# Four RMS norms of a decoder trunk's first stage: spreading the row factors by TensorE instead of through DRAM

## The chip, the cores and the metric

The kernel runs on one core of one Trainium2 chip. The time is the device time of one execution in microseconds (us); of several runs the median is given. All times inside the program come from one profiled execution and count from the start of its span.

## The reference

A decoder of two layers on 1024 tokens of 1024 channels, in float32. Only layer 0's attention matters here:

```
hn  = x * rsqrt(mean(x*x) + eps) * attn_norm
cq  = hn @ w_dq                    # 512 channels
ckv = hn @ w_dkv                   # 256 channels and a rotary key of 64
cqn = rmsnorm(cq) * q_norm         # feeds all queries, nope and rotary
ckn = rmsnorm(ckv[:256]) * kv_norm # feeds keys and values
kpe = rope(ckv[256:], positions)
```

After that come causal attention with 8 heads, an output projection, a gated feed-forward block, then a second layer with differential attention and another such block, and a last norm.

## The kernel before

Activations lie transposed: channels on the 128 partitions, tokens along the free axis, in two halves `f` of 512 tokens. Every matmul operand is split into a high and a low part (`xh`, `xl`; `wah`, `wal`), and three matmuls make one product.

The first stage multiplies `x`, scaled by its gain only, with the joined weights of `w_dq` and `w_dkv`. For each half there is a **pass**: eight groups `k` (one for each block of 128 channels), in each of which seven accumulators (`n` = 0 to 6: four for q, two for kv, one for the rotary key) get three matmuls of 128x512, 21 in all. Four accumulators lie in the PSUM pool `mm2`, three in `bank()`. ScalarE makes `xh`, VectorE `xl`.

The norm's factor is applied behind the matmuls, since a factor for a token commutes with them. It is made thus (class `Norm`): `add` squares blocks on ScalarE and sums them in `ss` (VectorE in the first pass, GpSimd in the second); `invert` sums over partitions with small TensorE matmuls (`psn<-ones,ss`), takes the mean (`ms`) and an inverse root by ten small VectorE instructions of 128x4 (`rsy`, `rsz`, `rst`). The result `y` (shown as `rsy`) holds token j x 128 + p at partition p, column j. But it is wanted along the free axis and the same on every partition. `spread` brings it there, in one of two ways:

- `fast` false: `store` writes `y` to DRAM (`rd`), `load` reads it back to all partitions as the SBUF tile `rms`. Both DMAs are issued on the queue of SyncE.
- `fast` true: four float32 matmuls with `y`'s column broadcast as weights and the identity as the moving operand write the factor to a PSUM bank, `psr`, and the users read it there.

In the first stage six norms are made. The norms over 1024 channels of either pass, and the norms of q and kv of the first half, use the DRAM way. Only the norms of q and kv of the second half (`f == 1` in `compressed`) spread by TensorE.

With the factor `r`, `compressed` empties the seven accumulators by VectorE (`craw = acc * r`, `kraw`), adds squares for the norms of q and kv, inverts and spreads those, and makes `cn = craw * gain * rr`, split into `cqh`, `cql`, `ckh`, `ckl`. It is a generator: the first half's steps are called between the groups of the second pass (`STEP`: at k=2 q's `invert`, at k=3 kv's, at k=4 q's `spread` and `cn`, at k=5 kv's with the rotary key). The pass's own norm is inverted and spread at k=5 in the first pass and k=6 in the second (`INV`). After the second pass `rotary` multiplies the rotary query weights with `cqh`, `cql` of the first half, 48 matmuls, then the second half's norms of q and kv follow, then `rotary` for the second half, which begins the second half's use of `cqh`.

All these norms use `norm_bank`, one PSUM bank that `psn` and `psr` take in turn; the second half's q and kv use `bank`. The sine and cosine tables are made by `trig_tables` during the first pass.

The order is not written out: within `nc.start()` and `nc.finish()` all operations are recorded and then put in order by a greedy list plan (`Plan.finish`) with a duration for each operation. It picks what can start earliest, ties by place in the code. This order is fixed when the program is built; on the chip each engine runs its own list in order. The later stages have plans of their own. Almost every instruction is issued by one helper, so the profile shows it as line L287, and tile names tell them apart.

Of the kernel before, what the change touches and what calls it, by code (L numbers as in the profile page):

```python
# [11 lines left out]
F32 = mybir.dt.float32  # L12
F32R = mybir.dt.float32r
I32 = mybir.dt.int32
AF = mybir.ActivationFunctionType
# [5 lines left out]
P = 128  # L21
D = 1024
S = 1024
HF = 512
# [346 lines left out]
def trunk(ctx: ExitStack, tc: tile.TileContext, A: dict):  # L371
    nc = Plan(tc)
# [16 lines left out]
    def gain(which, k):  # L389
        c = GAINS[which] + k  # L390
        return gains[:, c : c + 1]
# [9 lines left out]
    def bank(name="ps"):  # L401
        if nc.on:
            return nc.ask(banks[0], [P, HF], F32, name, banks[1].get(name))
        return mm.tile([P, HF], F32, name=name, tag="mm")
# [4 lines left out]
    def move(dst, src):  # L409
        nc.sync.dma_start(out=f32(dst), in_=f32(src))  # L410

    def split(dst_hi, dst_lo, src, scale=1.0, sub=None):
        nc.scalar.activation(dst_hi, src, AF.Copy, scale=scale)
        if isinstance(scale, float) and scale == 1.0:
            (sub or nc.vector).tensor_tensor(dst_lo, src, f32(dst_hi), ALU.subtract)
        else:
            nc.vector.scalar_tensor_tensor(dst_lo, src, scale, f32(dst_hi), ALU.mult, ALU.subtract)
# [45 lines left out]
    def early(place):  # L463
        return xa if place[0] == "x" else z1
# [8 lines left out]
    class Norm:  # L473
# [34 lines left out]
        def spread(self):  # L508
            if self.fast:
                r = self.bank("psr")  # L510
                for j in range(self.n):
                    nc.tensor.matmul(r[:, j * P : (j + 1) * P], lhsT=self.y[:, j : j + 1].to_broadcast([P, P]), rhs=ident, start=True, stop=True)
                return r
            return self.load(self.store(), self.tmp)

# [26 lines left out]
    with tc.using_default_side("right"):  # L542
# [8 lines left out]
    tmpa = Tags(lambda q: {"ss": norma, "r": norma, "craw": crawp, "t": norma}.get(q) or (wa_p if q[0] == "w" else early(q)), kraw=("z5",), ss=("ss",), r=("r",), craw=("craw",),  # L551
                t=("z6", "z7", "z8", "z9", "t", "t"), xh=[q + "h" for q in spare], xl=[q + "l" for q in spare],
                y=[f"wa{part}{k}" for k in range(4, 8) for part in "hl"], rot=[q + part for q in spare for part in "hl"])
# [57 lines left out]
    def causal_mask():  # L611
        nc.gpsimd.memset(mask, 0.0)
        nc.gpsimd.affine_select(
            out=mask[:, S - P :], in_=mask[:, S - P :], pattern=[[-1, P]], base=0, channel_multiplier=1,
            compare_op=ALU.is_ge, fill=NEG,
        )
# [4 lines left out]
    def load_x(f, k):  # L621
        x = xs.tile([P, HF], F32, name="x", tag="x")
        nc.sync.dma_start(out=x, in_=A["x"][f, k])
        return x
# [21 lines left out]
    def compressed(f, acc, r):  # L646


        tok = slice(f * HF, (f + 1) * HF)
        kinds = (("q", Q_LORA, 0, NQ, cqh, cql), ("kv", KV_LORA, NQ, NC_, ckh, ckl))  # L650
        norms, raws = [], []
        for which, dim, lo_n, n_t, _, _ in kinds:
            norms.append(Norm(tmpa, dim, fast=f == 1, bank=bank if f else norm_bank))
            for n in range(lo_n, lo_n + n_t):
                c = tmpa.tile([P, HF], F32, name="craw", tag="craw", bufs=6)
                nc.vector.tensor_tensor(c, acc[n], r, ALU.mult)
                norms[-1].add(c)
                raws.append(c)
        kraw = tmpa.tile([P, HF], F32, name="kraw", tag="kraw")
        nc.vector.tensor_tensor(kraw, acc[NA - 1], r, ALU.mult)  # L660
        for norm in norms:
            yield
            norm.invert()
        for norm, (which, _, lo_n, n_t, dst_h, dst_l) in zip(norms, kinds):
            yield
            rr = norm.spread()
            for n in range(n_t):
                t = tmpa.tile([P, HF], F32, name="cn", tag="t")
                nc.vector.scalar_tensor_tensor(t, raws[lo_n + n], gain(which, n), rr, ALU.mult, ALU.mult)
                split(dst_h[n][f], dst_l[n][f], t)  # L670
        m1 = tmpa.tile([P, HF], F32, name="m1", tag="t")
        m2 = tmpa.tile([P, HF], F32, name="m2", tag="t")
        nc.vector.tensor_tensor(m1[0:64], kraw[0:64], cs[0:64, tok], ALU.mult)
        nc.vector.tensor_tensor(m2[0:64], kraw[64:128], cs[64:128, tok], ALU.mult)
        nc.vector.tensor_tensor(m1[0:64], m1[0:64], m2[0:64], ALU.add)
        split(krh[0:64, tok], krl[0:64, tok], m1[0:64])
        for t in (krh, krl):
            move(t[64:128, tok], t[0:64, tok])
        yield
# [62 lines left out]

    for f in range(2):
        acc = [mm2.tile([P, HF], F32, name="acc", tag="mm2") for _ in range(4)] + [bank() for _ in range(3)]
        norm = Norm(tmpa, D, adder=nc.gpsimd if f else nc.vector, bank=norm_bank)
        after = []
        for k in range(KT):
            if (f, k) == TRIG:
                c4, s4, cs = trig_tables()
                causal_mask()  # L750
            if (f, k) in STEP:
                next(before, None)
            x = xt[k]
            xh = tmpa.tile([P, HF], F32R, name="xh", tag="xh")
            xl = tmpa.tile([P, HF], F32R, name="xl", tag="xl")
            split(xh, xl, x, scale=gain("attn0", k))
            for i in range(0 if k == 0 else k + LEAD, min(k + LEAD + 1, KT)):
                norm.add(xt[i])
            if k == INV[f]:
                norm.invert()  # L760
                r = norm.spread()
            if f == 0:
                after.append(load_x(1, k))
            for n in range(NA):
                cols = slice(n * P, (n + 1) * P)
                nc.tensor.matmul(acc[n], lhsT=wa_h[k][:, cols], rhs=xh, start=k == 0, stop=False)
                nc.tensor.matmul(acc[n], lhsT=wa_h[k][:, cols], rhs=xl, start=False, stop=False)
                nc.tensor.matmul(acc[n], lhsT=wa_l[k][:, cols], rhs=xh, start=False, stop=k == KT - 1)
        for _ in before:
            pass  # L770
        xt = after
        before = compressed(f, acc, r)
        next(before)
    ws = [rotary_weights(g) for g in range(2)]
# [1205 lines left out]
```

## Time and profile before

| | |
|---|---|
| median of 3 runs | 2520.44 us (2517.12 to 2521.76) |
| profiled execution | 2517.07 us |
| its span | 2515.0 us |
| its mean granted TensorE clock | 0.977 |
| matmuls busy | 2335.8 us |
| VectorE, ScalarE, GpSimd busy | 1929.2, 1164.3, 1125.1 us |

The first stage takes about the first 160 us of the span. Busy shares are means over the whole span; what holds a stage is read from its own waits and its own timeline. TensorE, VectorE, ScalarE and GpSimd are called PE, DVE, ACT and POOL in the rows, PEld is TensorE's weight load, and SPq is the queue of SyncE.

### The profile page before, as it was taken

How to read it: one execution, taken by the hardware profiler on the slowest of the kernel's cores; microseconds unless marked ns; L12 is line 12 of the kernel's file. 1: busy time of each engine (PE TensorE's matmuls, PEld its weight loads, DVE VectorE, ACT ScalarE, POOL GpSimd, SP SyncE). 2: the span in 40 equal slices, each digit the busy share in tenths (PEclk: the TensorE clock that was granted, in tenths of full speed). 3: DMA queues.
4: the chain of work that ended last, by engine and by line, in shares of the span. 5: the costliest groups of instructions: out<-in, count | busy, mean ns of one | idle time of the engine just before them, and what ended most of it. 6: DMA issues, size and time to landing. Idle time of an engine off the chain costs nothing. (4 is left out here: it accounts for less than half of the span.)

```text
span 2515.0 us, 38090 instructions
## 1 busy us (share of the span) xinstructions
PE 2335.8 (93%) x12744; PEld 1996.4 (79%) x12744; DVE 1929.2 (77%) x3685; ACT 1164.3 (46%) x2319; POOL 1125.1 (45%) x979
## 2 busy tenths in 40 slices
PE   8689999999899998999999999989989999988997
PEld 6579988778788886777788888878768888876777
DVE  6575555387887789999678677676598787789997
ACT  4246555244444444344355555554344444454442
POOL 2145652163555554123377674444264555542212
PEclk9899999999999998999999999999999999999999
DMA  5156665566332235332266663373744232244322
GB/s 182 22 158 203 197 199 177 163 214 202 111 92 72 84 104 179 92 105 92 87 201 198 207 196 113 106 233 125 251 142 154 79 93 72 85 147 149 103 66 73
DMA packets 204691, 347.41 MB, mean 138 GB/s; under 512 B 26832, under 2 KB 59856, under 8 KB 204496
## 3 DMA queue, kind: packets, MB, share of 16 engines
q1 hardware_dynamic: 204496, 344.99, 43.8%
q8 instruction: 101, 1.65, 0.3%
q14 instruction: 94, 0.77, 0.1%
HBM read 240.94 MB, written 95.04 MB: 134 GB/s over the span
## 5 line engine op out<-in xcount | busy, mean ns | idle before, releaser
L287 ACT ACTIVATE wh<-wr 128x512 fp32r<-128x512 f32 (+2 forms) x530 | 287.5, 550 | 450.1 <-PE pb L287 137.7
L287 DVE TENSOR_TENSOR wl<-wr,wh 128x512 fp32r<-128x512 f32 (+2 forms) x530 | 396.0, 761 | 38.6 <-ACT wh L287 38.0
L287 PE MATMUL pa<-xh,wh 128*128 128x512 f32 (+1 forms) x850 | 339.6, 401 | 35.9 <-DVE h L287 16.2
L287 PE MATMUL pa<-xh,wl 128*128 128x512 f32 (+1 forms) x850 | 337.3, 398 | 18.4 <-DVE wl L287 17.1
L287 PE MATMUL pa<-xl,wh 128*128 128x512 f32 (+1 forms) x850 | 336.6, 396 | 4.0 <-DVE xl L287 4.0
L287 PE MATMUL pb<-xh,wh 128*128 128x256 f32 (+1 forms) x976 | 293.7, 304 | 23.4 <-DVE s L287 17.4
L287 PE MATMUL pb<-xl,wh 128*128 128x256 f32 (+1 forms) x976 | 293.0, 301 | 0.0
L287 PE MATMUL pb<-xh,wl 128*128 128x256 f32 (+1 forms) x976 | 291.8, 301 | 0.0
L287 POOL TENSOR_TENSOR wr<-wr 128x512 f32<-128x512 f32 x128 | 179.6, 1403 | 172.6 <-DMA wr<-wgu 84.3
L287 POOL TENSOR_TENSOR xl<-stg,xh 128x512 fp32r<-128x512 f32 x66 | 110.9, 1698 | 305.3 <-ACT xh L287 159.0
L287 PEld LDWEIGHTS pa<-xh,wh 128*128 128x128 f32 x850 | 163.0, 192 | 77.5 <-DVE h L287 14.6
L287 PEld LDWEIGHTS pb<-xh,wh 128*128 128x128 f32 x976 | 187.6, 193 | 46.2 <-DVE s L287 26.6
L287 PEld LDWEIGHTS pa<-xh,wl 128*128 128x128 f32 x850 | 162.1, 191 | 57.0 <-DVE wl L287 24.8
L287 PEld LDWEIGHTS pb<-xl,wh 128*128 128x128 f32 x976 | 188.5, 193 | 13.7
L287 PEld LDWEIGHTS pb<-xh,wl 128*128 128x128 f32 x976 | 188.0, 193 | 6.0 <-DVE wl L287 0.5
L287 PEld LDWEIGHTS pa<-xl,wh 128*128 128x128 f32 x850 | 163.0, 192 | 34.4 <-DVE xl L287 5.7
L287 POOL TENSOR_SCALAR p<-p,tot 128x640 f32<-128x640 f32 (+7 forms) x128 | 98.9, 774 | 180.6 <-DVE tot L287 114.0
L287 ACT ACTIVATE p<-sc,nmax 128x128 f32<-128x128 f32 (+7 forms) x192 | 141.8, 740 | 77.6 <-DVE nmax L287 45.3
L287 POOL TENSOR_TENSOR qt<-wr 128x256 f32<-128x256 f32 x120 | 102.8, 876 | 124.8 <-DVE wl L287 107.2
L287 DVE TENSOR_TENSOR s<-s,pb 128x256 f32<-128x256 f32 (+1 forms) x278 | 115.6, 426 | 39.5 <-PE pb L287 36.6
L287 PE MATMUL pc<-xh,wh 128*128 128x512 f32 x352 | 139.1, 398 | 4.5 <-DVE h L287 4.3
L287 PE MATMUL pc<-xl,wh 128*128 128x512 f32 x352 | 138.9, 395 | 2.5 <-DVE xl L287 2.5
(295 smaller groups left out, 6491.2 us busy)
## 6 DMA issues: line engine op xcount, KB each, us to landing
wr<-wgu SPq DMA_DIRECT2D x142, 256.0 KB, 3.2
act_d<-s SPq DMA_DIRECT2D x88, 256.0 KB, 2.5
stg<-act_d SPq DMA_DIRECT2D x88, 256.0 KB, 2.9
wr<-wd SPq DMA_DIRECT2D x96, 192.0 KB, 2.4
pb<-wgu SPq DMA_DIRECT2D x60, 256.0 KB, 4.0
preh<-ph SPq DMA_DIRECT2D x58, 256.0 KB, 3.0
prel<-pl SPq DMA_DIRECT2D x58, 256.0 KB, 2.8
wh<-preh SPq DMA_DIRECT2D x58, 256.0 KB, 4.8
```

Of the source, the lines that this page charges most:

```text
L287: return getattr(getattr(self.nc, engine), name)(*map(put, args), **{k: put(a) for k, a in kw.items()})
```

## The change

`spread` gets a third way, `fast="sbuf"`: the four matmuls of the TensorE way, then one ScalarE copy of `psr` into the SBUF tile `rms`, which has the tag and the two buffers that `load` used. The four norms of the first stage that went through DRAM take this way. Users of `rms` are as they were. The norms of the second half's q and kv stay with `psr`, and no other stage's norm is touched.

```diff
                 r = self.bank("psr")
                 for j in range(self.n):
                     nc.tensor.matmul(r[:, j * P : (j + 1) * P], lhsT=self.y[:, j : j + 1].to_broadcast([P, P]), rhs=ident, start=True, stop=True)
+                if self.fast == "sbuf":
+                    t = self.tmp.tile([P, HF], F32, name="rms", tag="r", bufs=2)
+                    nc.scalar.activation(t, r, AF.Copy)
+                    return t
                 return r
             return self.load(self.store(), self.tmp)
...
-            norms.append(Norm(tmpa, dim, fast=f == 1, bank=bank if f else norm_bank))
+            norms.append(Norm(tmpa, dim, fast=True if f else "sbuf", bank=bank if f else norm_bank))
...
-        norm = Norm(tmpa, D, adder=nc.gpsimd if f else nc.vector, bank=norm_bank)
+        norm = Norm(tmpa, D, fast="sbuf", adder=nc.gpsimd if f else nc.vector, bank=norm_bank)
```

## Rows read from the trace of the kernel before

**Rows 1.** The page: busy time, and TensorE's granted clock in 40 slices.

```profile
PE 2335.8 (93%) x12744; PEld 1996.4 (79%) x12744; DVE 1929.2 (77%) x3685; ACT 1164.3 (46%) x2319; POOL 1125.1 (45%) x979
...
PEclk9899999999999998999999999999999999999999
```

**Rows 2.** View of waits, 30 to 160 us: total, times, longest.

```profile
DVE craw L287 <- DMA rms<-rd: 21.2, 2, 12.6
...
DVE cn L287 <- DMA rms<-rd: 14.4, 2, 11.1
```

**Rows 3.** Timeline of the queue of SyncE: start, us, what.

```profile
76.58 0.39 SPq L287 DMA_DIRECT2D rd<-rsy  x1
84.97 0.33 SPq L287 DMA_DIRECT2D rms<-rd  x1
85.39 0.38 SPq L287 DMA_DIRECT2D rd<-rsy  x1
97.03 0.32 SPq L287 DMA_DIRECT2D rms<-rd  x1
```

**Rows 4.** Timeline of VectorE; idle time before in brackets.

```profile
40.47 0.16 DVE L287 TENSOR_TENSOR rsy<-rsy,rsz 128x4 f32<-128x4 f32 x1
...
53.76 2.48 DVE L287 TENSOR_TENSOR craw<-acc,rms 128x512 f32<-128x512 f32 x4 [8.59 <-DMA rms<-rd]
...
75.42 1.13 DVE L287 TENSOR_TENSOR rsy<-rsy,rsz 128x4 f32<-128x4 f32 x1
...
80.57 0.16 DVE L287 TENSOR_TENSOR rsy<-rsy,rsz 128x4 f32<-128x4 f32 x1
91.88 2.74 DVE L287 SCALAR_TENSOR_TENSOR cn<-craw,gains,rms 128x512 f32<-128x512 f32 x4 [11.15 <-DMA rms<-rd]
...
100.85 1.42 DVE L287 SCALAR_TENSOR_TENSOR cn<-craw,gains,rms 128x512 f32<-128x512 f32 x2 [3.22 <-DMA rms<-rd]
...
103.01 0.75 DVE L287 SCALAR_TENSOR_TENSOR xl<-x,gains,xh 128x512 fp32r<-128x512 f32 x1
...
121.17 2.48 DVE L287 TENSOR_TENSOR craw<-acc,rms 128x512 f32<-128x512 f32 x4 [12.60 <-DMA rms<-rd]
```

**Rows 5.** Timeline of TensorE; idle time before in brackets.

```profile
54.59 0.77 PE L287 MATMUL acc<-xh,wah 128*128 128x512 f32 x1 [6.53 <-DVE craw L287]
...
58.55 0.39 PE L287 MATMUL acc<-xh,wah 128*128 128x512 f32 x1
...
61.81 0.40 PE L287 MATMUL ps<-xh,wal 128*128 128x512 f32 x1
...
66.24 1.00 PE L287 MATMUL psn<-ones,ss 128*128 128x64 f32 x8
...
103.82 0.80 PE L287 MATMUL acc<-xl,wah 128*128 128x512 f32 x1 [10.02 <-DVE xl L287]
...
109.85 0.39 PE L287 MATMUL ps<-xh,wah 128*128 128x512 f32 x1
...
122.01 0.77 PE L287 MATMUL psr<-cqh,wrh 128*128 128x512 f32 x1 [10.61 <-DVE craw L287]
...
126.81 0.39 PE L287 MATMUL psr<-cqh,wrl 128*128 128x512 f32 x1
...
138.24 1.16 PE L287 MATMUL psr<-ident,rsy 128*128 128x128 f32 x8 [0.85 <-DVE rsy L287]
139.69 1.13 PE L287 MATMUL psr<-ident,rsy 128*128 128x128 f32 x8 [0.29 <-DVE rsy L287]
141.99 1.20 PE L287 MATMUL psr<-cqh,wrh 128*128 128x512 f32 x4 [1.17 <-ACT cqh L287]
```

**Rows 6.** ScalarE: groups by form (busy us, mean ns, idle us before), then its timeline.

```profile
L287 ACT ACTIVATE kh<-psp 128x512 fp32r<-128x512 f32 x16 | 9.5, 597 | 10.2 <-PE psp L287 10.2
...
54.48 0.63 ACT L287 ACTIVATE ss<-craw 128x512 f32<-128x512 f32 x1 [9.90 <-DVE craw L287]
```

**Rows 7.** Timeline of GpSimd.

```profile
71.12 7.26 POOL L287 TENSOR_TENSOR ss<-ss,sq 128x512 f32<-128x512 f32 x5
```

## The prediction

> **What bounds the kernel now.** I read the page first: TensorE's matmuls are busy for 93% of the span, and its granted clock is below nine tenths in only two of 40 slices, the second being the one from 63 to 126 us [rows 1]. So the first stage differs from the rest. The view of waits names who is late there: VectorE's `craw` and `cn` wait 21.2 and 14.4 us for the load `rms<-rd` [rows 2]. The reader is to see one pattern three times in the timelines.
>
> First pass (token half 0): the inverse root `rsy` is ready at 40.47 + 0.16 = 40.63 us, and `craw`, its first user, starts at 53.76 us after 8.59 us of idle VectorE, released by `rms<-rd` [rows 4]. That is 13.1 us for a trip to DRAM and back. TensorE ended the pass at 54.59 - 6.53 = 48.06 us and stood still, since the next pass needs the accumulators that `craw` empties [rows 5].
>
> Norms of q and kv: the queue of SyncE issues store, load, store, load in order, at 76.58, 84.97, 85.39 and 97.03 us [rows 3]. A load can't start until its store has landed, 8.4 and 11.6 us later, and kv's store stands behind q's load, though kv's `rsy` was ready at 80.73 us. `cn` of q starts at 91.88, that of kv at 100.85, and queued behind them on VectorE is the `xl` of 103.01 that TensorE wants: idle 10.02 us [rows 4, 5].
>
> Second pass: the same trip once more, `craw` at 121.17, TensorE idle 10.61 us from 111.40 [rows 4, 5].
>
> After each gap matmuls come at half rate. Warm ones are (61.81 - 58.55)/14 = 0.233 us apart. After the gaps, nine take 54.59 to 58.55 (1.86 us more than 9 x 0.233), fourteen take 103.82 to 109.85 (2.77 more), eleven take 122.01 to 126.81 (2.24 more) [rows 5]. In these stretches TensorE is on the path that sets the end: idle and half rate are 27.16 + 6.87 = 34.0 us.
>
> **The change, part by part.** It removes four stores and four loads on SyncE's queue, and with them the trip from `rsy` to `rms`. It adds for each of the four norms four matmuls (recorded as eight) and one ScalarE copy PSUM to SBUF. The second half's q and kv norms already spread by TensorE: one spread of eight records took 1.16 us [rows 5]. The copy has no row of its own; a ScalarE copy of 128x512 out of PSUM into fp32r took 597 ns on average [rows 6]. So `rms` is there about 1.16 + 0.60 + 0.1 for hops = 1.9 us after `rsy`, not 13.1. The users still read SBUF, so their durations don't change. Nothing is moved by hand, but the stage's order is planned anew.
>
> The copies (4 x 0.6 = 2.4 us) I cost at nothing: ScalarE works in order and has gaps where they stand, such as 9.90 us before 54.48 [rows 6]. If that cover failed they would delay `craw` and `cn` by 0.6 us each, which delays TensorE only where an accumulator or an `xl` is then late. The norm bank of PSUM is a single one; each spread now holds it until its copy ends, 1.8 us, and the next user (a sum of squares one group, 21 x 0.233 = 4.9 us, on) comes later than that. The spreads on TensorE are not hidden: 1.16 each, bounds 1.13 to 1.16 by the two rows.
>
> The new wait: TensorE works in order, so a spread that stands in its queue before `rsy` is ready stops all matmuls behind it. Row by row:
>
> First norm: the nearest rows are the two spreads of the second half, for which TensorE waited 0.85 and 0.29 us [rows 5]. Mean 0.6, bounds 0 to 1.3.
>
> q: its sum of squares is on TensorE at 66.24 us, at the start of group k=2; `rsy` is ready at 75.42 + 1.13 = 76.55, 10.3 us later [rows 4, 5]. The code puts the spread at k=4, behind two groups and two sums: 2 x (4.9 + 1.0) = 11.8 us. Margin 1.5, so wait 0. kv: ready at 80.73, 14.5 us later; its spread stands at 11.8 + 1.16 + 4.9 = 17.9. Wait 0. Bounds for both together: 0 to 3.4.
>
> q's chain is slow because GpSimd adds squares at the same time (5 adds from 71.12 in 7.26 us): a 128x4 instruction that takes 0.16 us at 80.57 took 1.13 at 75.42 [rows 4, 7], and about every other one is slow, five of the ten. That speaks against the change, since TensorE is now behind this chain. The Trainium skill, "SBUF — State Buffer", section "Who interferes with whom", says that VectorE and GpSimd share a port pair by an exclusive lock, and who comes second blocks for the whole instruction. By that rule every instruction of the chain could lose an add's time; here only every other one did, so the trace agrees in part.
>
> Fourth norm (second pass): sum at k=6, when the adds are over; wait 0.6 as for the first, bounds 0 to 1.3. Its `rms` comes in time: `craw` needs the first accumulator's last matmul, about one group later.
>
> What is late next. First pass: `craw` 0 waits for its accumulator, whose last matmul is 18 x 0.233 = 4.2 us before the pass ends, so `craw` runs under the matmuls and no gap is left: 6.53 + 1.86 - 1.16 - 0.6 = 6.6 us gained. Second pass: the `cn` run soon after each spread, under matmuls, and the `xl` of k=7 is no longer behind a DMA: 10.02 + 2.77 - 3 x 1.16 - 0.6 = 8.7 us. After the second pass: today 111.40 to 141.99, 30.6 us, lie between its end and the first matmul that needs the second half's `cqh` [rows 5], of which 20.8 follow the start of `craw` at 121.17. With `craw` starting 4.2 us before the end, that matmul comes 20.8 - 4.2 = 16.6 us after it. TensorE's own work in between is 48 x 0.233 (rotary of the first half) + about 2 (sums) + 2.3 (spreads) = 15.5, so 16.6 stands: 30.6 - 16.6 = 14.0 gained. Bounds: 9.8 if the `craw` don't start until the pass ends, 15.1 if TensorE's work alone counts.
>
> Sum: 6.6 + 8.7 + 14.0 = **29.3 us**. By the bounds: (5.9 to 7.2) + (5.3 to 9.3) + (9.8 to 15.1) = 21 to 31.6. What follows starts from these results and has no clock of its own (one core runs alone), so it moves up as a whole. The profiled execution took 2517.07 us (span 2515.0): 2517.07 - 29.3 = 2487.8. The median of the runs is 3.4 higher, 2520.44, which gives 2491.1. I forecast **2490 us**, between them, nearer the median.
>
> **Rivals.** (a) *TensorE waits for the slowed chain.* If all ten instructions of q's chain are slow, five more by 1.0 us, `rsy` is ready 15.3 us after the sum against 11.8: wait 3.5, and kv's behind it some 2. With a further wait of that size at the fourth norm the gain is 20 to 25: 2495 to 2500. For it: the 1.13 us row. Against: the every-other pattern leaves a margin of 1.5. By the rule of "SBUF — State Buffer" in the Trainium skill, named above, this would be the case to expect. (b) *VectorE becomes the wait.* From q's sum to the end of the second pass, six groups or some 36 us with sums and spreads, it has to put the chains of q and kv with what lies between (14.5), six `cn` (2.74 us for four [rows 4], so 4.1), their six differences (about as much) and some 7 us for the fourth chain, `xl` and the rotary key. Should the plan put `xl` behind `cn` late again, or the fourth `rsy` come late, half of the second or third term stays: gain 12 to 20, 2500 to 2508. Against: that is about 30 of 36 us. (c) *No effect*: another input than `rms` would have come as late. Against: each wait in [rows 2] names the load, and the accumulators were done 5.7 us before `craw`. Gain under 5. (d) *Slower.* The new plan puts each spread right behind its own sum. Then TensorE stands through each chain: 76.55 - 67.24 = 9.3 us as for q, and goes to half rate, 2.8 more, 12.1 a norm and 48 for four, against 34.0 - 4.6 = 29.4 gained: 2539. It decides once the waits pass 29.4 us, 7.4 a norm. Against: the code asks for q's and kv's spreads two groups later, and the spreads in today's trace waited under 1 us.
>
> **How the numbers follow.** Forecast (gain 25 to 33) 0.70; (a) 0.13; (b) 0.10; (c) 0.03; (d) 0.04. About 0.2%, 5 us, is what a measurement of this kernel tells from no change. Faster: 0.70 + 0.13 + 0.10 and a little of (c), 0.94; same 0.03; slower 0.03, as (d) could end even. Range: from a gain of 33 on the profiled execution, 2484, through (a) into (b), a gain of 18 on the median, 2502.
>
> **What would show it.** No `rd` in the trace; four more groups of eight `psr<-ident,rsy`, and four ScalarE copies of about 0.6 us. No TensorE gap over 1.5 us between 12 and 95 us, full clock from 40 to 110 us; the second pass ending near 96 us, the first matmul on the second half's `cqh` near 113, not 141.99. Stages after it unchanged in length. I am wrong if TensorE shows idle time before `psr<-ident,rsy` of several us (a, d), if `xl` or `craw` still hold it (b), or if a later stage gives the time back.

## The result, and the profile of the changed kernel

The changed kernel took 2488.66 us, median of four runs (2486.97 to 2491.85), against 2520.43 us (2517.12 to 2521.76) for the kernel before on the same chip: a ratio of 0.9877, with a 95% interval from 0.986 to 0.9894. The forecast was 2490 us. By the medians the gain is 31.8 us, by the interval 26.7 to 35.3. The profiled execution took 2489.24 us, 27.8 us less than that of before, which at 2517.07 us is the fastest of its executions; so a comparison of the two profiles shows somewhat less than the medians do.

The page of the changed kernel, busy time and granted clock, against [rows 1]:

```profile
PE 2334.4 (94%) x12776; PEld 1998.5 (80%) x12776; DVE 1928.1 (78%) x3685; ACT 1167.5 (47%) x2323; POOL 1124.2 (45%) x979
...
PEclk9999999999999999999999999999999999999999
```

TensorE has 32 matmuls more (four spreads of eight records), ScalarE four instructions more, and the weak slice of the clock from 63 to 126 us is gone. (The other weak slice of before, from 943 to 1006 us, is gone too; it lies far behind this stage, and nothing here says why.) Busy times hardly moved: what went is idle time. Two of the six stores `rd<-rsy` are left, both in later stages (the forecast's sign, no `rd` at all, overlooked them), so no norm of this stage goes through DRAM. TensorE's timeline shows where the four spreads stand and what replaced the gaps of [rows 5] (start, us, what; idle time before in brackets):

```profile
40.20 1.05 PE L287 MATMUL psr<-ident,rsy 128*128 128x128 f32 x8
...
48.79 0.40 PE L287 MATMUL acc<-xh,wah 128*128 128x512 f32 x1
...
58.59 1.00 PE L287 MATMUL psn<-ones,ss 128*128 128x64 f32 x8
...
70.17 1.05 PE L287 MATMUL psr<-ident,rsy 128*128 128x128 f32 x8
70.97 0.48 PE L287 MATMUL acc<-xh,wah 128*128 128x512 f32 x1
71.29 0.40 PE L287 MATMUL acc<-xl,wah 128*128 128x512 f32 x1
...
75.96 1.05 PE L287 MATMUL psr<-ident,rsy 128*128 128x128 f32 x8
...
86.86 1.13 PE L287 MATMUL psr<-ident,rsy 128*128 128x128 f32 x8 [0.56 <-DVE rsy L287]
...
94.13 0.40 PE L287 MATMUL psr<-cqh,wrh 128*128 128x512 f32 x1
...
110.67 1.19 PE L287 MATMUL psr<-cqh,wrh 128*128 128x512 f32 x4
```

The second pass begins at 48.79 us and follows the first without a gap. The row of 94.13 us is the first matmul after the second pass, and that of 110.67 us the first on the second half's `cqh`. The one wait left is 0.56 us. The table by windows of the changed kernel (busy us of each engine, granted clock, DMA) says the same:

```profile
40.00:60.00 20.00, 20.00 (x96) 16.42 (x95) 12.10 (x23) 12.73 (x22) 0.00 (x0) 1.00 0.52 113
60.00:80.00 20.00, 20.00 (x100) 16.64 (x99) 19.44 (x36) 6.94 (x12) 9.85 (x7) 1.00 0.00 1
80.00:100.00 20.00, 19.44 (x94) 15.77 (x93) 14.57 (x33) 6.25 (x10) 0.00 (x0) 1.00 0.06 14
100.00:120.00 20.00, 20.00 (x102) 16.47 (x102) 19.56 (x49) 6.35 (x11) 5.08 (x4) 1.00 0.28 106
```

TensorE (first number behind the comma) is busy but for that wait, at the full clock (1.00, the upper of its two levels, 2.4 GHz), from 40 to 120 us. The new copies on ScalarE, then on VectorE the last instruction of q's root, the `craw` of the second pass and a user of TensorE's `psr` behind it:

```profile
41.30 0.60 ACT L287 ACTIVATE rms<-psr 128x512 f32<-128x512 f32 x1 [2.27 <-PE psr L287]
...
71.28 0.58 ACT L287 ACTIVATE rms<-psr 128x512 f32<-128x512 f32 x1
...
77.66 0.58 ACT L287 ACTIVATE rms<-psr 128x512 f32<-128x512 f32 x1
...
88.09 0.60 ACT L287 ACTIVATE rms<-psr 128x512 f32<-128x512 f32 x1 [4.57 <-PE psr L287]
```

```profile
67.77 1.13 DVE L287 TENSOR_TENSOR rsy<-rsy,rsz 128x4 f32<-128x4 f32 x1
...
90.20 2.72 DVE L287 TENSOR_TENSOR craw<-acc,rms 128x512 f32<-128x512 f32 x4 [3.49 <-PE acc L287]
...
99.93 0.69 DVE L287 TENSOR_TENSOR t<-psr,s 128x512 f32<-128x512 f32 x1 [1.51 <-PE psr L287]
```

`craw` of the second pass now waits for its accumulator, not for the load of [rows 4].

### The profile page after: what moved, and what is told of

Read it like the earlier page. It is cut to its first block, busy times and chain, and to the rows that moved or that the text cites. A ratio compares the mean times of both kernels' runs of the same rounds, so it can differ in the third digit from the quotient of the medians.

```text
span 2487.0 us, 38148 instructions
## 1 busy us (share of the span) xinstructions
PE 2334.4 (94%) x12776; PEld 1998.5 (80%) x12776; DVE 1928.1 (78%) x3685; ACT 1167.5 (47%) x2323; POOL 1124.2 (45%) x979
```

## The experiments

The code behind attention's start is the same in all kernels but e11, which changes one pair of instructions of the second head; yet the time from the fifth store of attention's output to the end of the span ran from 2295 to 2310 us in their profiled executions. So effects of a few us are read at three landmarks: the first matmul on the second half's `cqh`, the first matmul of attention's scores (`sc<-kh,qh`), and the fifth store of attention's output (`o_hi<-oh` on the queue of SyncE). They are the same work in every kernel. What TensorE has done before the first of them is not: in the changed kernel and in e1, e4, e5, e7, e8, e10 and e11 seven matmuls of the first head's projections stand ahead of it, in e9 two, in before, e2, e3 and e6 none. Starts in us, then the ratio to the kernel before on the same chip with its interval:

| kernel | `cqh` | score | fifth store | ratio |
|---|---|---|---|---|
| before | 141.99 | 161.48 | 219.82 | |
| changed | 110.67 | 130.84 | 191.22 | 0.9877 (0.986 to 0.9894) |
| e1, pass norms only | 126.15 | 146.31 | 204.87 | 0.9933 (0.9909 to 0.9957) |
| e2, q and kv only | 128.67 | 148.15 | 206.69 | 0.9932 (0.9913 to 0.9951) |
| e3, first pass only | 137.43 | 156.93 | 215.19 | 0.9968 (0.9954 to 0.9982) |
| e4, before with gaps filled | 141.38 | 161.56 | 221.19 | 1.0005 (0.9991 to 1.0019) |
| e5, spreads early | 115.90 | 136.07 | 194.40 | 0.9898 (0.9879 to 0.9917) |
| e6, e5 with VectorE's adds | 110.65 | 130.72 | 189.05 | 0.9879 (0.9862 to 0.9896) |
| e7, no copy for q and kv | 111.44 | 131.62 | 188.94 | 0.987 (0.9856 to 0.9885) |
| e8, low half by VectorE | 111.78 | 130.93 | 191.87 | 0.9865 (0.9848 to 0.9881) |
| e9, other buffers | 110.52 | 130.49 | 190.03 | 0.9865 (0.9838 to 0.9891) |
| e10, changed once more | 111.44 | 131.62 | 189.63 | 0.9864 (0.9844 to 0.9884) |
| e11, high half by GpSimd | 110.36 | 130.56 | 189.10 | 0.9869 (0.9839 to 0.99) |

**One part at a time.** e1 keeps the new way for the two pass norms and gives q and kv of the first half back to DRAM; e2 does the opposite; e3 keeps it for the first pass alone.

```diff
 e1, e3
-            norms.append(Norm(tmpa, dim, fast=True if f else "sbuf", bank=bank if f else norm_bank))
+            norms.append(Norm(tmpa, dim, fast=f == 1, bank=bank if f else norm_bank))
 e2
-        norm = Norm(tmpa, D, fast="sbuf", adder=nc.gpsimd if f else nc.vector, bank=norm_bank)
+        norm = Norm(tmpa, D, adder=nc.gpsimd if f else nc.vector, bank=norm_bank)
 e3
+        norm = Norm(tmpa, D, fast="" if f else "sbuf", adder=nc.gpsimd if f else nc.vector, bank=norm_bank)
```

> The two norms over 1024 channels spread by TensorE with a copy, the norms of q and kv of the first half go through DRAM again. Theory (each trip stood on TensorE's path by itself): only the middle gap comes back, 9.6 us by the trace after the change, so about 2498 us and one gap of about 10 us before the k=7 xl. Rival (the trips lean on each other through the orders of the engines): the fourth spread now stands in TensorE's order ahead of that xl, its rsy is queued on VectorE behind the late cn of kv, and TensorE stops there instead, for about 12 us and the half rate after it: 2502 us, the gap before psr<-ident,rsy.

> The norms of q and kv spread by TensorE, the two norms over 1024 channels go through DRAM as before. Theory: the first gap comes back in full (7.7 us). The last one comes back only in part, since rsy of the second pass is ready some 7 us before that pass ends and no longer behind the late cn: a trip of 12.5 us leaves a gap of about 5 instead of 10.6, and craw runs behind it, which costs 9.5 us; together 17 us, 2506 us. Rival (each trip has its own fixed price): 7.7 + 14 back, 2510 us.

> Only the norm of the first pass spread by TensorE, the other three through DRAM. Theory: the first gap and its half rate go, less one spread, 7.7 us by the trace after the change: 2512.7 us, with the middle and last gaps at 10 and 10.6 us as before. Rival (the gain of the first pass is swallowed by the next wait in line, the trip of q and kv): under 3 us, 2518 us or more.

In e1 TensorE's one long wait stands ahead of the fourth spread, and VectorE's timeline says why:

```profile
101.83 2.04 PE L287 MATMUL psr<-ident,rsy 128*128 128x128 f32 x8 [16.42 <-DVE rsy L287]
```

```profile
93.97 1.42 DVE L287 SCALAR_TENSOR_TENSOR cn<-craw,gains,rms 128x512 f32<-128x512 f32 x2 [6.00 <-DMA rms<-rd]
...
101.53 0.16 DVE L287 TENSOR_TENSOR rsy<-rsy,rsz 128x4 f32<-128x4 f32 x1
```

The chain of the second pass's norm is queued behind kv's `cn`, which still waits for its load; it ends at 101.53 + 0.16 = 101.69 us, and TensorE stands for 16.42 us. So a late kv holds the pass norm's spread as well, as the rival had it. The size agrees with the rival too: at the fifth store e1 is 13.65 us behind the changed kernel, where the rival's time stands for some 13 and the theory's for 9.6.

In e2 the two outer gaps are back and the middle one is gone; the loss at the fifth store, 15.5 us, is nearer to the theory's 17 than to the rival's 21.7. Of it 1.4 us are trips that took longer than in before (13.62 and 13.53 us from root to `craw`, against 13.13 and 12.60). The theory's last gap had the wrong size: the root was ready 5.9 us before the pass ended, not 7, and the gap is 8.40 us, not 5:

```profile
54.91 0.77 PE L287 MATMUL acc<-xh,wah 128*128 128x512 f32 x1 [6.64 <-DVE craw L287]
...
108.86 0.79 PE L287 MATMUL psr<-cqh,wrh 128*128 128x512 f32 x1 [8.40 <-DVE craw L287]
```

At the fifth store e1 gains 14.95 us and e2 13.13, together 28.1 of the 28.6 us of both (at the `cqh` landmark 29.2 of 31.3): within what the trips vary, the two halves of the change add up. e3 gains 4.6 us. q's sum of squares, which stands ahead of its first remaining trip, and kv's `cn` behind that trip:

```profile
59.80 1.00 PE L287 MATMUL psn<-ones,ss 128*128 128x64 f32 x8
```

```profile
95.42 1.42 DVE L287 SCALAR_TENSOR_TENSOR cn<-craw,gains,rms 128x512 f32<-128x512 f32 x2 [5.81 <-DMA rms<-rd]
```

At q's sum e3 is 66.24 - 59.80 = 6.4 us ahead of before, the changed kernel 7.7 us; the difference is the wait ahead of the first spread, 1.34 us in e3 and none in the changed kernel. Behind it e3's trips took 1.7 us longer than those of before: 21.15 us from kv's root to its `cn` against 20.12, and 13.26 us from the last root to `craw` against 12.60. So the first pass alone is worth 6.4 to 7.7 us, and the next trips do not swallow it, against the rival; they were only longer in this execution. By the median time e3 gains 8 us (4.5 to 11.6).

**The half rate after the gaps.** Behind the first and the last gap of before the granted clock is 0.50 (54.6 to 58.5 and 122.1 to 126.8 us), the lower of its two levels, 1.2 GHz: the half rate. e4 is the kernel before with useless matmuls into `norm_bank` behind each pass (24 and 40), so that TensorE is busy during most of the first and last gap.

```diff
+        fill = norm_bank("fill")
+        for i in range((24, 40)[f]):
+            nc.tensor.matmul(fill, lhsT=wa_h[KT - 1][:, :P], rhs=xh, start=True, stop=True)
```

> The kernel before, with all four trips through DRAM, and matmuls of no use put behind the first pass (24 of 128x512) and the second pass (40), so that TensorE works through most of the two gaps; nothing is left out. Theory (of the 34 us, 1.86 and 2.24 us are the half rate after these two gaps, the rest is the wait for the trip): the gaps stay as long, the matmuls after them come 0.233 us apart at once, 2516 us. Rival (the half rate is the greater part of what the change gives back): more than 8 us faster than before. If the filling itself delays the passes, slower than before.

```profile
48.01 5.76 PE L287 MATMUL fill<-xh,wah 128*128 128x512 f32 x24
55.21 0.47 PE L287 MATMUL acc<-xh,wah 128*128 128x512 f32 x1 [1.43 <-DVE craw L287]
...
111.56 9.50 PE L287 MATMUL fill<-xh,wah 128*128 128x512 f32 x40
123.22 0.56 PE L287 MATMUL psr<-cqh,wrh 128*128 128x512 f32 x1 [2.16 <-DVE craw L287]
```

After the first gap the full rate is there at once (granted clock 1.00 from 55.3 to 59.0 us), after the second it is not (0.43 us from matmul to matmul up to 126.57 us, granted clock 0.52 from 123.3 to 126.5). VectorE's timeline, first of before, then of e4, shows that the half rate after the last gap does cost something:

```profile
130.04 1.29 DVE L287 TENSOR_TENSOR t<-psr,s 128x512 f32<-128x512 f32 x2 [1.58 <-PE psr L287]
```

```profile
122.38 2.48 DVE L287 TENSOR_TENSOR craw<-acc,rms 128x512 f32<-128x512 f32 x4 [13.31 <-DMA rms<-rd]
...
130.64 0.69 DVE L287 TENSOR_TENSOR t<-psr,s 128x512 f32<-128x512 f32 x1 [0.38 <-PE psr L287]
```

In before VectorE stands 1.58 us for a `psr` that TensorE's matmuls at half rate finish late; in e4, with a shorter stretch at half rate, 0.38 us. The first matmul on the second half's `cqh` follows `craw` by 141.38 - 122.38 = 19.0 us, against 20.8 in before [rows 4, 5]; a part of that is the new order of e4, since the first score comes no earlier. Behind the first gap, from `craw` to q's root, e4 takes 21.6 us against 22.8. But the trips were longer in this execution (13.70 against 13.13 us from the first root to `craw`, 21.26 against 20.12 from kv's root to its `cn`, 13.31 against 12.60 ahead of the last `craw`), 2.4 us together, and whether the added matmuls have to do with that is not shown. In the time no gain is to be seen: the ratio is 1.0005, and its interval, 0.9991 to 1.0019, excludes the theory's gain of 4 us as well as the rival's of more than 8. So the half rate is a small part of what the change gives back, up to 1.2 us behind the first gap and 1.8 behind the last in the trace, and none of it shows in the time.

**Where the spreads stand.** e5 asks for q's and kv's spread right behind the inverse root, in place of two groups later; e6 does that and also lets VectorE add the second pass's squares, so that GpSimd is idle there.

```diff
 e5, e6
+            norm.rr = None if f else norm.spread()
...
-            rr = norm.spread()
+            rr = norm.spread() if f else norm.rr
 e6
-        norm = Norm(tmpa, D, fast="sbuf", adder=nc.gpsimd if f else nc.vector, bank=norm_bank)
+        norm = Norm(tmpa, D, fast="sbuf", bank=norm_bank)
```

> As after the change, but the spreads of q and kv of the first half are called right behind their inversion, two groups earlier in the code. Theory (a spread that stands in TensorE's order before rsy is ready stops all matmuls behind it, and rsy of q takes 10.3 us from its sum because GpSimd adds squares meanwhile): the plan puts q's spread 20 matmuls behind its sum, 5.5 us, so TensorE waits about 5 us there, perhaps with 2 us of half rate: 2494 to 2496 us. Rival (the place in the code does not matter, the wait is hidden by slack later in the stage): within 2 us of the changed kernel, 2487 to 2491.

> As e5, but VectorE, not GpSimd, adds the squares of the second pass, so that GpSimd is idle during the chains of q and kv. Theory (GpSimd's adds are what makes every other 128x4 instruction take 1.1 us): all ten instructions of q's chain take 0.15 to 0.17 us, rsy of q is ready before its spread, no gap there: 2488 to 2491 us. Rival (the slow instructions are slow by themselves, or VectorE's own seven adds of 0.6 us cost as much): 1.1 us instructions are still there, or the gap before the spread is, 2494 us or more.

TensorE and VectorE in e5:

```profile
58.30 1.00 PE L287 MATMUL psn<-ones,ss 128*128 128x64 f32 x8
...
68.67 2.04 PE L287 MATMUL psr<-ident,rsy 128*128 128x128 f32 x8 [4.65 <-DVE rsy L287]
```

```profile
64.52 0.16 DVE L287 TENSOR_TENSOR rst<-rst,rsz 128x4 f32<-128x4 f32 x1
64.72 1.11 DVE L287 SCALAR_TENSOR_TENSOR rsy<-rst,rsy 128x4 f32<-128x4 f32 x1
```

TensorE stands 4.65 us, the spread itself runs at half rate (granted clock 0.50 from 69.0 to 71.5 us), and the second half's `cqh` comes 5.2 us later than in the changed kernel. In e6 there is no wait, and the chain's instructions, from 62.44 to 68.48 us, take 0.15 or 0.16 us each:

```profile
70.07 1.05 PE L287 MATMUL psr<-ident,rsy 128*128 128x128 f32 x8
```

```profile
64.62 0.15 DVE L287 TENSOR_TENSOR rst<-rst,rsz 128x4 f32<-128x4 f32 x1
...
65.35 0.15 DVE L287 SCALAR_TENSOR_TENSOR rsy<-rst,rsy 128x4 f32<-128x4 f32 x1
```

So GpSimd's adds make the slow instructions: 1.11 us beside them, 0.15 us without. But e6 is not clean on TensorE's wait. Its plan knew of VectorE's adds, which stand between the chain's instructions, and put the spread 10.7 us after the sum's start, not 5.7. The root is ready 9.3 us after the sum's start there (68.48 + 0.15 - 59.38) and 10.2 us in e5 (67.42 + 1.10 - 58.30): as the rival expected, VectorE's own adds cost almost as much. Of the wait of 4.65 us the faster chain thus accounts for about 1 us; it is the place of the spread that took the rest away. The Trainium skill, "SBUF — State Buffer", section "Who interferes with whom", says that VectorE and GpSimd share a port pair by an exclusive lock, and that VectorE instructions with two SBUF inputs, or in a two-port mode, contend for it. That the slow rows come with GpSimd's adds agrees; that the same `rst<-rst,rsz` with two inputs takes 0.16 us beside them does not follow from it, so the trace agrees in part.

**The copy.** In e7 q's and kv's `cn` read the factor from PSUM, without ScalarE's copy.

```diff
-            norms.append(Norm(tmpa, dim, fast=True if f else "sbuf", bank=bank if f else norm_bank))
+            norms.append(Norm(tmpa, dim, fast=True, bank=bank if f else norm_bank))
```

> As after the change, but the norms of q and kv of the first half are spread without the ScalarE copy: cn reads the factor from PSUM. Theory (the copy is off the path): cn takes 0.74 us either way, but the one norm bank is held until the last cn of q, about 1 us after kv's spread could start, so TensorE waits about 1 us: 2488 to 2491 us, no measurable change. Rival (the copy's 0.6 us and its hops are on the path): 2 to 3 us faster than the changed kernel, 2486.

```profile
77.47 1.13 PE L287 MATMUL psr<-ident,rsy 128*128 128x128 f32 x8 [1.09 <-DVE cn L287]
```

The bank is held until `cn` has read it, and kv's spread waits 1.09 us. The second half's `cqh` comes 52.6 us after q's sum (58.85 to 111.44), against 52.1 in the changed kernel and in its repeat e10: 0.5 us later, not the 2 to 3 us earlier of the rival, and no difference in time can be measured. The copy costs nothing that shows here, and it frees the bank.

**The start of attention.** 31.3 us gained at the `cqh` landmark have become 28.6 us at the fifth store. Four kernels look for the rest. In the changed kernel TensorE waits 1.94 us for GpSimd's low half of the first head's key weights, then runs at half rate (granted clock 0.50 from 127.8 to 129.0 us):

```profile
126.21 0.50 PE L287 MATMUL psp<-ckh,wlo 128*128 128x512 f32 x1 [1.94 <-POOL wlo L287]
...
127.77 0.63 PE L287 MATMUL psp<-ckh,whi 128*128 128x512 f32 x1
...
146.24 0.39 PE L287 MATMUL psv<-whi,ckh 128*128 128x256 f32 x1 [1.84 <-DVE vl L287]
...
148.66 0.63 PE L287 MATMUL sc<-kh,qh 128*128 128x512 f32 x1
```

e8 makes that low half on VectorE, e9 puts the weights in buffers that are free earlier, and e10 is the changed kernel again, without an edit.

```diff
 e8
...
-        st["wk"] = weight(A["wuk"][0], NC_ * P, "k")
+        st["wk"] = weight(A["wuk"][0], NC_ * P, "k", sub=nc.vector)
 e9
+        st["wk"] = weight(A["wuk"][0], NC_ * P)
```

> As after the change, and the low part of the first head's key weights, made just before attention, is taken by VectorE instead of GpSimd, which is the wait of 1.94 us that TensorE has at 126 us of the changed trace, before a stretch at half rate. Theory (that wait is on the path): the gap there goes, and with it some of the half rate, 2 to 4 us faster than the changed kernel, 2485 to 2487 us. Rival (VectorE, busy 19.6 of 20 us from 100 to 120, is late instead): no change, 2488 to 2490.

> The changed kernel, with the high and low half of the first head's key weights in another pair of buffers, which nothing of the first stage occupies, so that TensorE need not wait for GpSimd's low half (1.94 us at the projection that uses it) when it starts that head's keys. What is looked at is when the fifth store of attention's output stands on SyncE's queue, 219.82 us before and 191.22 us in the changed kernel. Theory: the wait of 1.94 us and the half rate behind it are the place where about 2.8 us of the gain are given back; without them the fifth store comes at 187 to 189.5 us, and the time is 2485 to 2489 us, which is within the spread of the rest of the kernel. Rival: the wait moves to the next thing that TensorE needs (the rotated queries or keys, or the low half again, since GpSimd makes it behind the same work as before); the store stays at 190 to 192 us.

> The changed kernel once more, without an edit. Theory: what is given back at the start of attention depends on short waits there after which TensorE falls to half rate or not, and this differs between executions; the fifth store of attention's output, at 191.22 us in the first trace, comes anywhere between 188.5 and 191.5 us. Rival: it is fixed by the order of the instructions; the store comes at 191.2 us within 0.3 us, with the same two waits ahead of it. For either the time is 2484 to 2495 us and the ratio to the kernel before 0.985 to 0.990.

e8 waits 2.76 us for VectorE's `wlo`; its first score follows the `cqh` landmark by 19.15 us, 1.0 us less than in the changed kernel (20.17), but the fifth store is no earlier. e9 has no wait there, but 3.48 us for ScalarE's `qh` ahead of the first score, which comes 0.35 us earlier. In both the rival is right as far as the fifth store goes: the next thing is late. Nor does the half rate behind this wait set the first score: in e5 and e11, which run the projections behind the same wait at full rate, the stretch is 20.17 and 20.20 us. e10 decides more than they do: the same instructions in the same order gave the fifth store 1.6 us earlier, at 189.63 us, with 0.85 us of waiting ahead of the `psv` row, not 1.84, and no half rate behind it. The rival, that the order alone fixes it, falls.

What times the `psv` row is in ScalarE's timeline; the row of e10, which comes to this place 0.8 us later and finds the load landed at the same time, stands under that of the changed kernel:

```profile
144.16 0.63 ACT L287 ACTIVATE whi<-wraw 128x512 fp32r<-128x512 f32 x1 [2.14 <-DMA wraw<-wuqn]
144.69 0.67 ACT L287 ACTIVATE p<-sc,nmax 128x512 f32<-128x512 f32 x1
```

```profile
144.12 0.64 ACT L287 ACTIVATE whi<-wraw 128x512 fp32r<-128x512 f32 x1 [1.16 <-DMA wraw<-wuqn]
```

ScalarE waits there for the second head's query weights, and a softmax row (144.69) and the copy `vh` (145.36), from which VectorE makes `vl`, are queued behind. That `psv` follows the `whi` row by 2.08 us in the changed kernel (144.16 to 146.24) and in before (174.30 to 176.38), by 2.09 in e10 and by 2.08 to 2.09 in e1, e2, e3, e5, e6, e7 and e8; in e4 and e9 TensorE shows no wait there. The load takes 7.3 us from its issue (136.86) in the changed kernel, 6.45 in e10 and 6.8 in before. e11 takes ScalarE out of this:

```diff
...
-                st["wq"] = weight(A["wuqn"][h], NQ * P)
+                st["wq"] = weight(A["wuqn"][h], NQ * P, hi=nc.gpsimd if h == 1 else None)
```

> The changed kernel, with the high part of the second head's query weights made by GpSimd and not by ScalarE, so that in ScalarE's queue no instruction that waits for that load's landing (144.16 us in the changed kernel, 144.12 in its repeat) stands ahead of a softmax row and of the copy that the first value projections need. Theory: in nine traces the value projection that waits follows ScalarE's first use of this load by 2.08 to 2.09 us, so the landing of the load is what times this place; with the use moved, that projection no longer stands 2.1 us behind the landing, its wait (1.84 and 0.85 us) is gone, and the fifth store of attention's output comes at 187.5 to 189.5 us, not 189.6 to 191.2. Rival: the pairing is a coincidence of the order, and what times the place is VectorE's or GpSimd's own work there; the value projection waits as before or GpSimd, which now stands behind the load, holds the softmax rows that it scales; the store comes at 189.6 us or later. The time is 2485 to 2495 us for either.

ScalarE's and TensorE's timelines in e11:

```profile
141.03 0.69 ACT L287 ACTIVATE p<-sc,nmax 128x512 f32<-128x512 f32 x1
...
146.10 0.63 ACT L287 ACTIVATE ph<-pt 128x512 fp32r<-128x512 f32 x1 [3.46 <-DMA preh<-ph]
```

```profile
142.53 0.28 PE L287 MATMUL psv<-whi,ckh 128*128 128x256 f32 x1
...
147.81 0.38 PE L287 MATMUL psv<-whi,ckh 128*128 128x256 f32 x1 [1.77 <-DVE vl L287]
```

The softmax row comes 3.7 us earlier than in the changed kernel and the value projections no longer wait for the load, as the theory said. But ScalarE then waits 3.46 us for another transfer, `preh<-ph`, and TensorE 1.77 us for the next `vl`. The fifth store, 189.10 us, is within the theory's range, 2.1 us earlier than in the changed kernel but only 0.5 earlier than in e10. So a transfer that ScalarE's queue stands behind does time this place; when one is taken away, the next does. That this is worth anything at the fifth store is not shown, since two executions of the changed kernel differ there by 1.6 us. No version beats the changed kernel by what can be measured: the intervals of e6 to e11 all contain its ratio.

## Why the prediction was right

The forecast of 2490 us holds, and so does the mechanism in the main; two of its steps came out right partly by luck. By its own steps:

- **The trip.** In the first pass the root is ready at 39.82 + 0.15 = 39.97 us and `rms` at 41.30 + 0.60 = 41.90 us: 1.9 us, as forecast, against 13.1 by DRAM.
- **First term, 6.6 us forecast, 7.7 measured.** The tenth matmul of the second pass moved from 58.55 [rows 5] to 48.79 + 9 x 0.233 = 50.89 us. The wait of 0.6 us did not occur in this execution. Of the ten traces with this spread five show no wait there and five one of 0.97 to 1.40 (the repeat e10 1.32, which leaves it 6.9 us at q's sum); so the bounds of 0 to 1.3 were about right, and 0.6 was a mean between two outcomes. The spread was priced too high: the matmul behind it starts 0.8 us after it, as at 70.17 and 70.97, and comes back to the 0.233 pace 0.09 later, so a spread costs TensorE about 0.9 us, not the 1.16 of its record. The records of pipelined matmuls overlap.
- **Second term, 8.7 forecast, 9.6 measured** (111.40 - 94.13 = 17.3, less 7.7). Three spreads at 0.9 in place of 1.16 give 0.8 of the difference. q and kv did not wait: q's root is ready at 68.90 us, its spread stands at 70.17, a margin of 1.3 us where 1.5 was worked out. The fourth norm waited 0.56, forecast 0.6. (The term's lower bound is not summed as its parts say: with both waits at their upper bounds, 3.4 and 1.3, it is 4.6, not 5.3, and the gain's 20, not 21. Nothing hangs on it.)
- **Third term, 14.0 forecast, 14.0 measured.** From the end of the second pass to the first matmul on the second half's `cqh` it is 110.67 - 94.13 = 16.5 us, forecast 16.6, before 30.6. `craw` starts 3.9 us before the pass ends, forecast 4.2, and `cqh` follows it by 20.5 us, forecast 20.8. But the 20.8 us were taken for work that simply moves with `craw`, and they hold the 1.58 us that VectorE stood for TensorE's `psr` (130.04, above). At 0.233 us those 24 matmuls would have ended at about 127.8 us, before VectorE came to them at 128.46: the half rate was on the path here, and the change took it away. The term still fits, because VectorE waits as long at the same place for another reason, which the forecast did not have: `craw` now starts before the pass ends, and those matmuls do not. That wait is 1.51 us (ahead of the row of 99.93 above), and that the two are of one size is luck.
- **All moves up as a whole.** This step was a little off. Of the 31.3 us at the `cqh` landmark 30.6 are left at the first score, 30.1 at that `psv`, 28.6 at the fifth store. The first 0.7 go with an order that puts seven matmuls of the first head's projections ahead of the landmark and then lets TensorE wait 1.94 us where it waited 0.68 before: from the `cqh` landmark to the first score it is 20.2 us in every kernel with that order but e8, e4 with its old trips among them, and 19.5 in before, e2 and e3. The next 0.5 are the longer landing of one load, and the last 1.5 come with the half rate after the wait of 1.84 us, which the repeat doesn't have: there 30.2 of 30.6 us are left at the fifth store. The terms that were too small (1.1 + 0.9 us) and this loss (2.7 us) nearly cancel, which is luck: 29.3 us forecast, 28.6 at the fifth store, 27.8 between the profiled executions. By the medians it is 31.8, and the 3 us between that and the fifth store are within the interval and not explained by any trace.
- **Rivals.** (a) and (d) have their mechanism: e5 shows TensorE standing 4.65 us behind a chain slowed by GpSimd as soon as the spread is asked for two groups earlier. In the changed kernel the code's distance, 11.6 us from sum to spread, keeps it off by 1.3 us. (b) did not come: VectorE is busy 19.44 of 20 us from 60 to 80, yet each `xl` came in time. Its other half, a late fourth root, did come in e1, but behind a load in VectorE's queue and not by VectorE's work. (c) is excluded, each half of the change (e1, e2) gaining 13 to 15 us alone.

## What to carry to other kernels

A small vector that is wanted across all partitions need not go through memory: four small matmuls and a copy took 1.9 us in place of a 13 us trip, and the gain is the time that TensorE and VectorE, working in order, stood behind the loads. Ask for such a spread far enough behind its sum that the chain is done, because an in-order TensorE stops with it. Price pipelined matmuls by the distance to the next start, and look for a gain at landmarks after each stage, since the later stages vary by more than a small edit is worth.

## What the hardware showed beyond what was expected

- A store issued right behind a load takes longer. From the issue of a 2 KB store `rd<-rsy` to that of the load that waits for it, kv's store, which goes out 0.4 us behind q's load, took 11.6 us in before and 11.0 to 12.2 in e1, e3 and e4; the other stores of these traces and of e2 took 8.2 to 9.7. Why is not shown. The same transfer also differs between executions: the load `wraw<-wuqn` took 6.45 us and 7.3 us in two executions of one kernel.
- Short idle stretches of TensorE can be followed by half rate, and their length alone does not decide. Ahead of the same matmul of scores, a wait of 1.74 us in before was followed by half rate at once (granted clock 0.50 from 168 to 171 us), one of 1.75 us in the changed kernel was not (1.00 from 138.5 to 144.0 us), and one of 2.54 us in e11, a little earlier, was not either (1.00 from 130.9 to 134.0 us). Likewise the wait of 1.94 us for the key weights was followed by half rate 1.6 us later in the changed kernel, and in e5 the rate stayed full (1.00 from 131.5 to 133.5 us). What TensorE did before each of them differs, and no run separates the two. The rows of before, of the changed kernel and of e11:

```profile
167.98 0.69 PE L287 MATMUL sc<-kh,qh 128*128 128x384 f32 x1 [1.74 <-ACT p L287]
```

```profile
138.19 0.44 PE L287 MATMUL sc<-kh,qh 128*128 128x384 f32 x1 [1.75 <-ACT p L287]
```

```profile
130.56 0.49 PE L287 MATMUL sc<-kh,qh 128*128 128x128 f32 x2 [2.54 <-ACT qh L287]
```
